# State space stage: tables in small portions, recurrence on VectorE, output units behind the last heads

## The chip, the cores and the metric

The kernel runs on one core of one Trainium2 chip. The metric is the device time of one execution in microseconds (us). All matrices are float32; each product is made of three matmuls on a rounded high part and the rest (`hi`, `lo`), so that weights are split on the chip before they are used.

## The reference

Two blocks of a model on 512 tokens of width 1024. The change lies in the first block's state space mixer (S5): 32 groups of 16 channels, each with 64 complex states.

```
proj = rmsnorm(x) @ w_in                  # u (512 wide), then q, k, v (512 each)
lam_bar = exp(lam * dt);  b_bar = ((lam_bar - 1) / lam) * b
states  = scan over tokens of  s = lam_bar * s + b_bar u
y = gelu(Re(c . states) + d * u)
y = y * sigmoid(y @ w_glu + b_glu)
mixed = concat(rmsnorm(y), rmsnorm(chunked_attention(q, k, v)))
x = x + mixed @ w_out;  x = x + FFN(rmsnorm(x));  x = rmsnorm(x)
```

Behind it come four layers of a second block, each with a mixer, attention on a memory of 256 vectors, and an FFN. The keys and values of that memory, for all four layers, are computed early in the kernel, between u and the first heads.

## The kernel before

The program is a list of units. A unit is 12 matmuls: four 128x128 weight tiles of one output tile, three matmuls each (`mm`, L185, L187, L189; 512 columns, 256 for the memory). Weights come in order through three buffers `raw` on SP's DMA queue, and are split two units ahead into `hi` (ScalarE, L233) and `lo` (VectorE, L235). Work beside the units is written as Python generators. Those in `self.gens` go one step on after each unit, those in `self.fine` one step after each matmul of a unit; a `yield` ends a step. The order in which instructions are issued this way is their priority; the tile framework then orders each engine's static queue by priority and by when it expects operands to be ready, so that an engine with nothing better to do takes later work early.

The units of the first block, counted from 0: 0 to 7 are u (four output tiles of two units), 8 to 39 the memory's keys and values (32 units), then heads in four pairs j of six units each (q, k, v), then w_out, and the FFN. The four units of GLU (`ssm_units`) stand before pair j = `SSM_AT`.

S5 runs in chunks of eight tokens beside these units:

- `s5_tables` (in `gens`): some 80 small VectorE operations on 16 to 64 columns, then `bb` (input matrices, 256 columns), powers `pw` of lam_bar up to 8, the block-diagonal `bd`, `L` (powers up to 64), and four blocks `A` of six operations on 512 columns (`cmul`, two of the blocks on GpSimd), turned by TensorE (L1224) into `Ain`.
- `s5_u`: copies u from PSUM, scales it by the norm (L1239) and stores it to DRAM.
- `s5_main` (in `fine`): waits for the tables, loads u, computes the chunks' states S (L1319, 128 small matmuls), then runs the recurrence over them, 14 steps of three operations on GpSimd (L1339 to L1341), `S5_STEP` matmuls apart.
- `s5_toeps` (in `fine`, beside the recurrence): clears two Toeplitz tiles, and for four parts m makes the powers F (`s5_powers`, 12 operations of 288 columns, L1260 to L1265), multiplies them (L1287), and spreads the result through DRAM into the Toeplitz tile (eight DMAs, L1299).
- `s5_main`, second part: `S5_WAIT` matmuls after both, four outputs: S is copied by GpSimd into S2 (L1352), 32 matmuls (L1358 with F, L1366 with the Toeplitz tile), y goes by way of `s5x` to DRAM (L1374, L1377). F for m = 2 and 3 is made a second time here, for half of it on GpSimd.

`s5x` has one buffer; F and A share two. `ssm_begin` ends whatever of `s5_main` is left, loads y turned and applies GELU (L1397); GLU's results are multiplied, squared, normed (L289, L323) and split again (`ssm_out`) before w_out can use them. `att_done` drains all generators before w_out.

Of the kernel before, what the change touches and what calls it, by code (L numbers as in the profile page):

```python
# [98 lines left out]
class Kern:  # L99
# [979 lines left out]
    def s5_tmp(self):  # L1079
        return self.s5.tile([P, T], F32, tag="s5x", name="s5x")  # L1080

    def s5_tables(self):
# [51 lines left out]
        dt = stt(acc, 1.0, kj.bitcast(F32), add, mul)  # L1134
        re, im = tt(lr, dt, mul), tt(li, dt, mul)
# [7 lines left out]
        r = ts(r, 3.1415925, -3.1415925, ALU.min, ALU.max)  # L1143
        s1, sh = new(16), new(16)
# [4 lines left out]
        em1 = stt(th, 2.0, rec, mul, mul)  # L1149
        mag = ts(em1, 1.0, None, add, ALU.bypass)  # L1150
# [13 lines left out]
        V.tensor_copy(out=pw[:, 1, :, 1:2], in_=ai.unsqueeze(2))  # L1164
        t = new(64).rearrange("p (a b) -> p a b", a=16)

        def cmul(out_r, out_i, xr, xi, yr, yi, t, eng):
            eng.tensor_tensor(out=out_r, in0=xr, in1=yr, op=mul)
            eng.tensor_tensor(out=t, in0=xi, in1=yi, op=mul)
            eng.tensor_tensor(out=out_r, in0=out_r, in1=t, op=sub)  # L1170
            eng.tensor_tensor(out=out_i, in0=xr, in1=yi, op=mul)
            eng.tensor_tensor(out=t, in0=xi, in1=yr, op=mul)
            eng.tensor_tensor(out=out_i, in0=out_i, in1=t, op=add)

        for lo, w in ((1, 1), (2, 2), (4, 4)):
            b = [pw[:, c, :, lo:lo + 1].to_broadcast([P, 16, w]) for c in (0, 1)]
            cmul(pw[:, 0, :, lo + 1:lo + 1 + w], pw[:, 1, :, lo + 1:lo + 1 + w],
                 pw[:, 0, :, 1:1 + w], pw[:, 1, :, 1:1 + w], b[0], b[1], t[:, :, :w], V)
# [5 lines left out]
        cmul(bb[:, 0], bb[:, 1], br, bi, w3[0], w3[1], t, V)  # L1184
        bd = pool.tile([P, 2, 16, 32], F32, tag="bd", name="bd")
        nc.gpsimd.memset(bd, 0.0)
        for c in range(2):
            for q in range(2):
                rows = slice(64 * q, 64 * q + 64)
                V.tensor_copy(out=bd[rows, c, :, 16 * q:16 * q + 16], in_=bb[rows, c])  # L1190
        pv = tail[:, 512:].rearrange("p (c a b) -> p c a b", c=2, a=16)
        for j in range(8):
            V.tensor_copy(out=pv[:, :, :, j:j + 1], in_=pw[:, :, :, 7 - j:8 - j])

# [4 lines left out]
        for w in (1, 2, 4):  # L1199
            b = [L[:, c, 0, :, w - 1:w].to_broadcast([P, 16, w]) for c in (0, 1)]  # L1200
            cmul(L[:, 0, 0, :, w:2 * w], L[:, 1, 0, :, w:2 * w], L[:, 0, 0, :, :w], L[:, 1, 0, :, :w],
                 b[0], b[1], t[:, :, :w], V)
# [7 lines left out]
        for m in range(4):  # L1210
            A = pool.tile([P, 2, 4, 9, 16], F32, tag="big", name="A", bufs=2)[:, :, :, 0:8]
            js = slice(4 * m, 4 * m + 4)
            x = [bb[:, c, js].unsqueeze(2).to_broadcast([P, 4, 8, 16]) for c in range(2)]
            y = [pv[:, c, js].unsqueeze(3).to_broadcast([P, 4, 8, 16]) for c in range(2)]
            t = (self.s5_tmp() if m % 2 else self.tmp()).rearrange("p (a b c) -> p a b c", a=4, b=8)
            cmul(A[:, 0], A[:, 1], x[0], x[1], y[0], y[1], t, G if m % 2 else V)
# [12 lines left out]
            yield  # L1229

    def s5_u(self, m, ps, norm):

        nc = self.nc
        t = self.tmp()
        turned = t.rearrange("p (t c) -> p c t", t=8)
        src = ps.rearrange("p (c t) -> p c t", t=8)

        nc.scalar.activation(out=turned, in_=src, func=ACTF.Copy)
        nc.vector.tensor_tensor(  # L1239
            out=turned, in0=turned, in1=self.bc(norm).rearrange("p (c t) -> p c t", t=8), op=ALU.mult,  # L1240
        )
# [5 lines left out]
    def s5_powers(self, m, split=(False, False)):  # L1247

        nc = self.nc
        cr, ci = self.s5_c  # L1250
        F = self.s5.tile([P, 2, 4, 9, 16], F32, tag="big", name="F", bufs=2)
        for q in range(2):
            js, ls = slice(4 * m + 2 * q, 4 * m + 2 * q + 2), slice(2 * q, 2 * q + 2)
            shape = [P, 2, 9, 16]
            x = [v[:, js].unsqueeze(2).to_broadcast(shape) for v in (cr, ci)]
            y = [self.s5_pw[:, c, js].unsqueeze(3).to_broadcast(shape) for c in range(2)]
            G = nc.gpsimd if split[q] else nc.vector
            t = (self.s5_tmp() if q else self.tmp())[:, :288]
            t = t.rearrange("p (a b c) -> p a b c", a=2, b=9)
            G.tensor_tensor(out=F[:, 0, ls], in0=x[0], in1=y[0], op=ALU.mult)  # L1260
            G.tensor_tensor(out=t, in0=x[1], in1=y[1], op=ALU.mult)
            G.tensor_tensor(out=F[:, 0, ls], in0=F[:, 0, ls], in1=t, op=ALU.subtract)
            G.tensor_tensor(out=F[:, 1, ls], in0=x[0], in1=y[1], op=ALU.mult)
            G.tensor_tensor(out=t, in0=x[1], in1=y[0], op=ALU.mult)
            nc.vector.scalar_tensor_tensor(  # L1265
                out=F[:, 1, ls], in0=F[:, 1, ls], scalar=-1.0, in1=t, op0=ALU.mult, op1=ALU.subtract
            )
        return F

    def s5_toeps(self):  # L1270
# [3 lines left out]
        for pair in (1, 0):  # L1274
            toep = self.toep[pair] = pool.tile([P, 8, 2, P], F32, tag="tab", name="toep", bufs=2)
            nc.vector.memset(toep, 0.0)
            k_dram = self.k_dram[pair]
            for m in range(2):
                ms = slice(8 * pair + 4 * m, 8 * pair + 4 * m + 4)
                F = self.powers[2 * pair + m] = self.s5_powers(2 * pair + m)  # L1280
# [11 lines left out]
                kt = self.s5_tmp()[:32].rearrange("p (j c) -> p j c", j=4)  # L1292
# [11 lines left out]
    def s5_main(self, tables):  # L1304
        nc = self.nc
        while tables in self.gens:
            yield
# [4 lines left out]
        S, G, L = self.S, nc.gpsimd, self.s5_L  # L1312
# [37 lines left out]
        for m in range(4):  # L1350
# [26 lines left out]
            nc.sync.dma_start(out=self.y_dram[m].rearrange("p g c -> p (g c)"), in_=y)  # L1377
            yield
# [94 lines left out]
    def first(self):  # L1473
# [12 lines left out]
        def squares():  # L1486
# [9 lines left out]
            self.finish(st["norm"]["gen"])  # L1496
# [291 lines left out]
```

## Time and profile before

| | us |
|---|---|
| three runs | 3168.74 median, 3168.13 to 3169.31 |
| the profiled execution | 3168.23 |
| its span, first to last instruction | 3166.3 |
| TensorE busy in the span | 3097.5 (98%) |
| VectorE busy | 1757.6 (56%) |
| GpSimd busy | 562.2 (18%) |

PE is TensorE, PEld its weight loads, DVE VectorE, ACT ScalarE, POOL GpSimd, SP the queue that issues the DMAs. Busy times of TensorE overlap from one matmul to the next. PEclk is the clock granted to TensorE as a share of 2.4 GHz, averaged over the stretch.

### The profile page before, as it was taken

Reading aid. Unit: us, or ns where it says so; the run is one execution under the profiler, and the core shown is the slowest. Engines: PE = TensorE matmul, PEld = TensorE weight load, DVE = VectorE, ACT = ScalarE, POOL = GpSimd, SP = SyncE. Lnnn points to the kernel's source line nnn. Section 1 sums busy time; section 2 is a strip of 40 time slices with the busy share of each in tenths; the row PEclk is TensorE's granted clock in tenths of the full one; section 3 lists DMA queues with packets and bytes.
Section 4 is the critical chain, followed back from the end, with each engine's and each line's share of the span. In section 5 each row is a group of like instructions: output and inputs, shape, how many; then the busy total and the mean of one; then the engine's idle time right before and its main releaser. Section 6 shows DMA issues by size and latency. Waiting matters only on the chain.

```text
span 3166.3 us, 39145 instructions
## 1 busy us (share of the span) xinstructions
PE 3097.5 (98%) x14664; PEld 2587.2 (82%) x14664; DVE 1757.6 (56%) x2979; ACT 1347.9 (43%) x2488; POOL 562.2 (18%) x464
## 2 busy tenths in 40 slices
PE   7899999999999999999999999999999999999998
PEld 6687788888888888888888888887888888878886
DVE  8977644458755344566753445655444477554444
ACT  5365423347754232455432334334333467542332
POOL 2731201032212010111110001112000123120103
PEclk9899999999999999999999999999999999999999
DMA  6432223332223323322233333233333322132332
GB/s 210 111 99 80 93 93 97 98 98 62 67 75 104 100 90 103 94 77 80 70 104 99 91 102 94 88 95 98 94 97 98 98 67 67 62 105 93 97 98 79
DMA packets 101694, 295.29 MB, mean 93 GB/s; under 512 B 22496, under 2 KB 26592, under 8 KB 101472
## 3 DMA queue, kind: packets, MB, share of 16 engines
q1 hardware_dynamic: 101504, 292.79, 30.4%
q8 instruction: 115, 1.88, 0.2%
q14 instruction: 75, 0.61, 0.1%
HBM read 286.20 MB, written 6.55 MB: 92 GB/s over the span
## 4 chain that ended last, share of the span: by engine, by line
PE 91%; DVE 6%; issue 1%; ACT 1%; DMA 1%; POOL 0%; SPq 0%; DVEq 0%; ACTq 0%; POOLq 0%
PE g L185 27%; PE g L189 27%; PE g L187 27%; DVE lo L235 1%; PE a L224 1%; PE a L225 1%; PE a L223 1%; DVE x L414 1%; PE z L722 1%; PE z L735 1%; PE a L289 0%; PE a L635 0%; PE z L187 0%; PE z L185 0%; PE z L189 0%
## 5 line engine op out<-in xcount | busy, mean ns | idle before, releaser
L233 ACT ACTIVATE hi<-raw 128x512 fp32r<-128x512 f32 (+2 forms) x1094 | 662.3, 607 | 1430.7 <-PE g L187 1330.4
L235 DVE TENSOR_TENSOR lo<-raw,hi 128x512 fp32r<-128x512 f32 (+2 forms) x1094 | 765.7, 701 | 653.8 <-ACT hi L233 643.7
L185 PE MATMUL g<-xh,hi 128*128 128x512 f32 x2720 | 1067.7, 393 | 12.2 <-ACT hi L233 7.8
L189 PE MATMUL g<-xh,lo 128*128 128x512 f32 x2720 | 1064.7, 392 | 0.0
L187 PE MATMUL g<-xl,hi 128*128 128x512 f32 x2720 | 1064.0, 391 | 0.0
L185 PEld LDWEIGHTS g<-xh,hi 128*128 128x128 f32 x2720 | 513.1, 189 | 119.8 <-ACT hi L233 7.8
L189 PEld LDWEIGHTS g<-xh,lo 128*128 128x128 f32 x2720 | 512.7, 188 | 105.2 <-issue 0.2
L187 PEld LDWEIGHTS g<-xl,hi 128*128 128x128 f32 x2720 | 512.9, 189 | 103.3
L189 PE MATMUL g<-ah,lo 128*128 128x512 f32 x1110 | 433.6, 391 | 3.1 <-DVE lo L235 2.7
L185 PE MATMUL g<-ah,hi 128*128 128x512 f32 x1110 | 432.0, 390 | 2.0 <-ACT t L271 2.0
L187 PE MATMUL g<-al,hi 128*128 128x512 f32 x1110 | 432.2, 389 | 0.0
L427 POOL TENSOR_TENSOR t<-t,bc 128x512 f32<-128x512 f32 x110 | 143.2, 1302 | 1405.2 <-ACT t L426 1405.2
L189 PEld LDWEIGHTS g<-ah,lo 128*128 128x128 f32 x1110 | 208.3, 188 | 50.8 <-DVE lo L235 8.0
L185 PEld LDWEIGHTS g<-ah,hi 128*128 128x128 f32 x1110 | 208.4, 188 | 45.3 <-ACT t L271 2.8
L187 PEld LDWEIGHTS g<-al,hi 128*128 128x128 f32 x1110 | 208.4, 188 | 43.1
L398 DVE TENSOR_TENSOR t<-g,bc 128x512 f32<-128x512 f32 x182 | 125.1, 688 | 173.7 <-PE g L189 169.5
L414 DVE TENSOR_TENSOR x<-x,g 128x512 f32<-128x512 f32 x151 | 103.4, 685 | 136.2 <-PE g L189 136.2
L429 DVE TENSOR_TENSOR t<-g,t 128x512 f32<-128x512 f32 x110 | 76.1, 692 | 180.3 <-PE g L189 160.4
L272 POOL TENSOR_TENSOR acc<-acc,t 128x512 f32<-128x512 f32 x82 | 114.9, 1405 | 335.9 <-ACT t L271 319.8
L233 ACT ACTIVATE ah<-t 128x512 fp32r<-128x512 f32 x110 | 69.5, 632 | 45.8 <-DVE t L429 45.8
L426 ACT ACTIVATE t<-t 128x512 f32<-128x512 f32 x110 | 69.7, 634 | 33.4 <-DVE t L398 33.3
L235 DVE TENSOR_TENSOR al<-t,ah 128x512 fp32r<-128x512 f32 x110 | 76.1, 692 | 12.0 <-ACT ah L233 2.3
(341 smaller groups left out, 3048.0 us busy)
## 6 DMA issues: line engine op xcount, KB each, us to landing
raw<-in_weights_dram SPq DMA_DIRECT2D x436, 512.0 KB, 3.5
raw<-in_weights_dram SPq DMA_DIRECT2D x76, 448.0 KB, 3.3
raw<-in_weights_dram SPq DMA_DIRECT2D x18, 384.0 KB, 3.2
x<-in_xT_dram SPq DMA_DIRECT2D x16, 256.0 KB, 3.6
x<-in_att_bias_dram SPq DMA_DIRECT2D x8, 256.0 KB, 6.0
kv<-kv SPq DMA_DIRECT2D x32, 64.0 KB, 2.4
out_dram<-x SPq DMA_DIRECT2D x8, 256.0 KB, 2.1
mraw<-in_memT_dram SPq DMA_DIRECT2D x2, 512.0 KB, 6.2
```

Of the source, the lines that this page charges most:

```text
L185: nc.tensor.matmul(out=out, lhsT=wh, rhs=xh, start=u.first and i == 0, stop=False)
L187: nc.tensor.matmul(out=out, lhsT=wh, rhs=xl, start=False, stop=False)
L189: nc.tensor.matmul(out=out, lhsT=wl, rhs=xh, start=False, stop=u.last and i == len(u.ks) - 1)
L223: nc.tensor.matmul(out=out, lhsT=ah, rhs=bh, start=start, stop=False)
L233: nc.scalar.activation(out=hi, in_=src, func=ACTF.Copy)
L235: eng.tensor_tensor(out=lo, in0=src, in1=hi.bitcast(F32), op=ALU.subtract)
L272: nc.gpsimd.tensor_tensor(out=norm["acc"][rows, :n], in0=norm["acc"][rows, :n], in1=sq[rows, :n], op=ALU.add)
L398: nc.vector.tensor_tensor(out=t, in0=ps, in1=bc, op=ALU.mult)
L414: self.nc.vector.tensor_tensor(out=self.x[m], in0=self.x[m], in1=ps, op=ALU.add)
L426: nc.scalar.activation(out=tg, in_=tg, func=ACTF.Silu)
L427: nc.gpsimd.tensor_tensor(out=tg, in0=tg, in1=self.bc(n), op=ALU.mult)
L429: nc.vector.tensor_tensor(out=h, in0=ps, in1=tg, op=ALU.mult)
```

## The change

`s5_tables` gives its operations out in some 37 steps instead of 11 (a `yield` after every few), `cmul` becomes a generator. `s5_powers` makes F in six operations of 576 columns on VectorE, `S5_PACE` = 6 matmuls apart, with the sign of c's imaginary part turned once in the tables. The recurrence's three operations go from GpSimd to VectorE, 14 matmuls apart instead of 10. The Toeplitz tiles are cleared by GpSimd. u is copied into x[4+m] and scaled as soon as the norm is there, and the norm is no longer forced to an end in `squares`. The GLU units stand behind all four head pairs (`SSM_AT` 4). With the same rule of counting, the tables end after unit 41 (before: 15).

```
-S5_STEP = 10
-S5_FILL = (24, 0)
-S5_POOL = (False, True)
+S5_STEP = 14
+S5_FILL = (12, 0)
+S5_PACE = 6
-SSM_AT = 3
+SSM_AT = 4
     def s5_tmp(self):
-        return self.s5.tile([P, T], F32, tag="s5x", name="s5x")
+        return self.s5.tile([P, 576], F32, tag="s5x", name="s5x")
     def s5_tables(self):
         f = stt(k, 2.12194440054690583e-4, f, mul, add)
+        yield
...
-        def cmul(out_r, out_i, xr, xi, yr, yi, t, eng):
+        def cmul(out_r, out_i, xr, xi, yr, yi, t, eng, pace=False):
             eng.tensor_tensor(out=out_r, in0=xr, in1=yr, op=mul)
             eng.tensor_tensor(out=t, in0=xi, in1=yi, op=mul)
+            if pace:
+                yield
...
-        cmul(bb[:, 0], bb[:, 1], br, bi, w3[0], w3[1], t, V)
+        yield from cmul(bb[:, 0], bb[:, 1], br, bi, w3[0], w3[1], t, V, True)
+        yield
+        V.tensor_scalar(out=ci, in0=ci, scalar1=-1.0, scalar2=None, op0=mul)
...
     def s5_u(self, m, ps, norm):
-        t = self.tmp()
+        t = self.x[4 + m]
         nc.scalar.activation(out=turned, in_=src, func=ACTF.Copy)
+        while norm["bc"] is None:
+            yield
...
+    def s5_powers(self, m, store, key):
+        F = store[key] = self.s5.tile([P, 2, 4, 9, 16], F32, tag="big", name="F", bufs=2)
+        js, shape = slice(4 * m, 4 * m + 4), [P, 4, 9, 16]
+        t = self.s5_tmp().rearrange("p (a b c) -> p a b c", a=4, b=9)
+        for c, op in ((0, ALU.add), (1, ALU.subtract)):
+            V.tensor_tensor(out=F[:, c], in0=x[c], in1=y[0], op=ALU.mult)
+            yield from wait(S5_PACE)
+            V.tensor_tensor(out=t, in0=x[1 - c], in1=y[1], op=ALU.mult)
+            yield from wait(S5_PACE)
+            V.tensor_tensor(out=F[:, c], in0=F[:, c], in1=t, op=op)
+            yield from wait(S5_PACE)
...
     def s5_toeps(self):
-            nc.vector.memset(toep, 0.0)
+            nc.gpsimd.memset(toep, 0.0)
-                F = self.powers[2 * pair + m] = self.s5_powers(2 * pair + m)
+                yield from self.s5_powers(2 * pair + m, self.powers, 2 * pair + m)
+                F = self.powers[2 * pair + m]
...
     def s5_main(self, before):
-            G.tensor_tensor(out=pr, in0=src.to_broadcast(shape), in1=fac, op=ALU.mult)
-            G.tensor_tensor(out=pr[:, :, 0:16], in0=pr[:, :, 0:16], in1=pr[:, :, 16:32], op=ALU.add)
-            G.tensor_tensor(out=dst, in0=dst, in1=pr[:, :, 0:16], op=ALU.add)
+            V.tensor_tensor(out=pr, in0=src.to_broadcast(shape), in1=fac, op=ALU.mult)
+            V.tensor_tensor(out=pr[:, :, 0:16], in0=pr[:, :, 0:16], in1=pr[:, :, 16:32], op=ALU.add)
+            V.tensor_tensor(out=dst, in0=dst, in1=pr[:, :, 0:16], op=ALU.add)
             yield from wait(S5_STEP)
...
-            if m < 2:
-                self.powers[m + 2] = self.s5_powers(m + 2, S5_POOL)
             nc.sync.dma_start(out=self.y_dram[m].rearrange("p g c -> p (g c)"), in_=y)
+            if m < 2:
+                yield from self.s5_powers(m + 2, self.powers, m + 2)
             yield
...
         def squares():
             self.begin_norm(st["norm"], D, 1e-6, gap=0)
-            self.finish(st["norm"]["gen"])
             yield
...
         def u_post(m, ps):
-            self.s5_u(m, ps, st["norm"])
+            st["u", m] = self.spawn(self.s5_u(m, ps, st["norm"]))
+            next(st["u", m], None)
             if m == 3:
-                st["s5"] = self.spawn(self.s5_main(st["tables"]), self.fine)
+                before = [st["u", k] for k in range(4)] + [st["tables"]]
+                st["s5"] = self.spawn(self.s5_main(before), self.fine)
```

## Rows read from the trace of the kernel before

**Rows 1.** The page: busy time, share of the span and instructions of each engine.

```profile
PE 3097.5 (98%) x14664; PEld 2587.2 (82%) x14664; DVE 1757.6 (56%) x2979; ACT 1347.9 (43%) x2488; POOL 562.2 (18%) x464
```

**Rows 2.** Busy time by stage: length, engines (instructions), PEclk, DMA share, GB/s.

```profile
0.00:50.00 50.00, 30.82 (x122) 24.98 (x122) 42.86 (x139) 28.72 (x50) 15.04 (x16) 0.91 0.63 216
50.00:85.00 35.00, 34.15 (x268) 33.94 (x268) 33.57 (x64) 15.32 (x27) 12.28 (x9) 0.93 0.64 196
85.00:143.00 58.00, 43.57 (x362) 37.64 (x361) 54.75 (x68) 15.81 (x26) 43.78 (x37) 0.85 0.40 103
143.00:226.00 83.00, 81.64 (x480) 69.84 (x478) 67.47 (x140) 49.40 (x104) 32.83 (x33) 1.00 0.36 105
226.00:273.00 47.00, 41.11 (x200) 34.39 (x200) 33.94 (x59) 35.54 (x61) 11.00 (x8) 0.96 0.27 79
273.00:335.00 62.00, 58.23 (x263) 47.76 (x264) 46.76 (x87) 29.05 (x60) 11.55 (x8) 0.94 0.26 81
...
380.00:400.00 20.00, 20.00 (x90) 16.54 (x89) 8.86 (x14) 7.59 (x12) 2.57 (x2) 1.00 0.30 92
```

**Rows 3.** Waits of TensorE, 0 to 362 us: total, times, longest.

```profile
PE a L323 <- DVE t L309: 11.4, 2, 6.2
...
PE s5ps L1287 <- DVE F L1265: 7.6, 3, 5.7
```

**Rows 4.** Groups of VectorE, 60 to 140 us: busy, mean ns, idle before.

```profile
L235 DVE TENSOR_TENSOR lo<-raw,hi 128x512 fp32r<-128x512 f32 x30 | 29.0, 977 | 1.1 <-ACT hi L233 1.1
...
L551 DVE TENSOR_TENSOR kvt<-g,membc 128x256 f32<-128x256 f32 x14 | 5.7, 410 | 0.0
...
L1276 DVE MEMSET toep<- 128x2048 f32 x2 | 3.5, 1765 | 0.7 <-issue 0.7
```

**Rows 5.** Groups of VectorE, 360 to 500 us.

```profile
L235 DVE TENSOR_TENSOR lo<-raw,hi 128x512 fp32r<-128x512 f32 x52 | 35.8, 688 | 40.7 <-ACT hi L233 40.7
```

**Rows 6.** One line, L1265: count, shortest/median/longest ns, first and last start.

```profile
L1265 DVE SCALAR_TENSOR_TENSOR F<-F,t x6: 444/764/1760, 89.3 to 197.5; 128x288 f32<-128x288 f32 x6
```

**Rows 7.** Groups of GpSimd, 0 to 230 us.

```profile
L1339 POOL TENSOR_TENSOR pr<-S,s5p 128x512 f32<-128x512 f32 x14 | 20.7, 1480 | 6.0 <-ACT S L1325 5.0
L1341 POOL TENSOR_TENSOR S<-S,pr 128x256 f32<-128x256 f32 x14 | 14.6, 1043 | 0.9
L1340 POOL TENSOR_TENSOR pr<-pr 128x256 f32<-128x256 f32 x14 | 14.0, 999 | 1.1
...
L272 POOL TENSOR_TENSOR acc<-acc,t 128x512 f32<-128x512 f32 x3 | 4.0, 1337 | 5.2 <-ACT t L271 5.2
```

**Rows 8.** TensorE in order of time, the memory's units: start, duration.

```profile
57.06 0.28 PE L185 MATMUL g<-memh,hi 128*128 128x256 f32 x1
57.18 0.28 PE L187 MATMUL g<-meml,hi 128*128 128x256 f32 x1
...
130.18 0.28 PE L189 MATMUL g<-memh,lo 128*128 128x256 f32 x1
```

**Rows 9.** SP's queue in order of time.

```profile
162.42 4.83 SPq L1299 DMA_DIRECT2D toep<-k_dram  x8
```

**Rows 10.** TensorE in order of time, the first S5 output.

```profile
171.02 0.61 PE L1358 MATMUL s5ps<-S,F 128*128 128x128 f32 x4
...
174.14 0.56 PE L1366 MATMUL s5ps<-U,toep 128*128 128x64 f32 x4
```

**Rows 11.** All engines in order of time, from the last S5 output to w_out.

```profile
218.45 0.60 ACT L1374 ACTIVATE s5x<-s5ps 128x512 f32<-128x512 f32 x1 [1.77 <-PE s5ps L1366]
...
227.90 0.99 PE L185 MATMUL g<-yh,hi 128*128 128x512 f32 x3 [1.96 <-ACT yh L233]
...
246.20 0.40 PE L189 MATMUL g<-yh,lo 128*128 128x512 f32 x1
...
273.15 1.65 PE L185 MATMUL g<-yh,hi 128*128 128x512 f32 x3 [2.56 <-ACT yh L233]
```

More of the change, by code (lines that the diff above doesn't have):

```diff
@@ L1143, in s5_tables @@
         r = ts(r, 3.1415925, -3.1415925, ALU.min, ALU.max)
+        yield
         s1, sh = new(16), new(16)
@@ L1149, in s5_tables @@
         em1 = stt(th, 2.0, rec, mul, mul)
+        yield
         mag = ts(em1, 1.0, None, add, ALU.bypass)
@@ L1154, in s5_tables @@
         ar = tt(tt(em1, cos, mul), cm1, add)
+        yield
         den = tt(tt(lr, lr, mul), tt(li, li, mul), add)
@@ L1157, in s5_tables @@
         V.reciprocal(out=rec, in_=den)
+        yield
         wr = tt(tt(tt(ar, lr, mul), tt(ai, li, mul), add), rec, mul)
+        yield
         wi = tt(tt(tt(ai, lr, mul), tt(ar, li, mul), sub), rec, mul)
+        yield
         pw = keep(2, 16, 9)
@@ L1164, in s5_tables @@
         V.tensor_copy(out=pw[:, 1, :, 1:2], in_=ai.unsqueeze(2))
+        yield
         t = new(64).rearrange("p (a b) -> p a b", a=16)
-        def cmul(out_r, out_i, xr, xi, yr, yi, t, eng):
+        def cmul(out_r, out_i, xr, xi, yr, yi, t, eng, pace=False):
             eng.tensor_tensor(out=out_r, in0=xr, in1=yr, op=mul)
             eng.tensor_tensor(out=t, in0=xi, in1=yi, op=mul)
+            if pace:
+                yield
             eng.tensor_tensor(out=out_r, in0=out_r, in1=t, op=sub)
             eng.tensor_tensor(out=out_i, in0=xr, in1=yi, op=mul)
+            if pace:
+                yield
             eng.tensor_tensor(out=t, in0=xi, in1=yr, op=mul)
@@ L1176, in s5_tables @@
             b = [pw[:, c, :, lo:lo + 1].to_broadcast([P, 16, w]) for c in (0, 1)]
-            cmul(pw[:, 0, :, lo + 1:lo + 1 + w], pw[:, 1, :, lo + 1:lo + 1 + w],
-                 pw[:, 0, :, 1:1 + w], pw[:, 1, :, 1:1 + w], b[0], b[1], t[:, :, :w], V)
+            yield from cmul(pw[:, 0, :, lo + 1:lo + 1 + w], pw[:, 1, :, lo + 1:lo + 1 + w],
+                            pw[:, 0, :, 1:1 + w], pw[:, 1, :, 1:1 + w], b[0], b[1], t[:, :, :w], V)
+            yield
         tail = pool.tile([P, 3 * 256], F32, tag="kt", name="tail")
@@ L1190, in s5_tables @@
                 V.tensor_copy(out=bd[rows, c, :, 16 * q:16 * q + 16], in_=bb[rows, c])
+        yield
         pv = tail[:, 512:].rearrange("p (c a b) -> p c a b", c=2, a=16)
@@ L1193, in s5_tables @@
             V.tensor_copy(out=pv[:, :, :, j:j + 1], in_=pw[:, :, :, 7 - j:8 - j])
+        yield
         L = self.s5p[:, 48:560].rearrange("p (a c b k) -> p a c b k", a=2, c=2, b=16)
@@ L1200, in s5_tables @@
             b = [L[:, c, 0, :, w - 1:w].to_broadcast([P, 16, w]) for c in (0, 1)]
-            cmul(L[:, 0, 0, :, w:2 * w], L[:, 1, 0, :, w:2 * w], L[:, 0, 0, :, :w], L[:, 1, 0, :, :w],
-                 b[0], b[1], t[:, :, :w], V)
+            yield from cmul(L[:, 0, 0, :, w:2 * w], L[:, 1, 0, :, w:2 * w], L[:, 0, 0, :, :w],
+                            L[:, 1, 0, :, :w], b[0], b[1], t[:, :, :w], V)
+            yield
         V.tensor_scalar(out=L[:, 0, 1], in0=L[:, 1, 0], scalar1=-1.0, scalar2=None, op0=mul)
@@ L1214, in s5_tables @@
             y = [pv[:, c, js].unsqueeze(3).to_broadcast([P, 4, 8, 16]) for c in range(2)]
-            t = (self.s5_tmp() if m % 2 else self.tmp()).rearrange("p (a b c) -> p a b c", a=4, b=8)
-            cmul(A[:, 0], A[:, 1], x[0], x[1], y[0], y[1], t, G if m % 2 else V)
+            t = (self.s5_tmp()[:, :T] if m % 2 else self.tmp()).rearrange("p (a b c) -> p a b c", a=4, b=8)
+            yield from cmul(A[:, 0], A[:, 1], x[0], x[1], y[0], y[1], t, G if m % 2 else V, m % 2 == 0)
             yield
@@ L1238, in s5_u @@
         nc.scalar.activation(out=turned, in_=src, func=ACTF.Copy)
+        while norm["bc"] is None:
+            yield
         nc.vector.tensor_tensor(
@@ L1245, in s5_u @@
         )
-    def s5_powers(self, m, split=(False, False)):
-        nc = self.nc
+    def s5_powers(self, m, store, key):
+        V = self.nc.vector
         cr, ci = self.s5_c
[L1251 to L1268, printed above, removed]
+        F = store[key] = self.s5.tile([P, 2, 4, 9, 16], F32, tag="big", name="F", bufs=2)
+        js, shape = slice(4 * m, 4 * m + 4), [P, 4, 9, 16]
+        x = [v[:, js].unsqueeze(2).to_broadcast(shape) for v in (cr, ci)]
+        y = [self.s5_pw[:, c, js].unsqueeze(3).to_broadcast(shape) for c in range(2)]
+        t = self.s5_tmp().rearrange("p (a b c) -> p a b c", a=4, b=9)
[6 more added lines that the diff above has]
+            yield from wait(S5_PACE)
     def s5_toeps(self):
@@ L1291, in s5_toeps @@
                         yield
-                kt = self.s5_tmp()[:32].rearrange("p (j c) -> p j c", j=4)
+                kt = self.s5_tmp()[:32, :T].rearrange("p (j c) -> p j c", j=4)
                 nc.scalar.activation(out=kt, in_=ps, func=ACTF.Copy)
@@ L1302, in s5_toeps, with s5_main @@
                 )
-    def s5_main(self, tables):
+    def s5_main(self, before):
         nc = self.nc
-        while tables in self.gens:
+        while any(g in self.gens for g in before):
             yield
@@ L1311, in s5_main @@
         )
-        S, G, L = self.S, nc.gpsimd, self.s5_L
+        S, G, V, L = self.S, nc.gpsimd, nc.vector, self.s5_L
         G.memset(S[:, :, :, 0:1], 0.0)
@@ L1370, in s5_main @@
                     yield
-            if m < 2:
-                self.powers[m + 2] = self.s5_powers(m + 2, S5_POOL)
-            y = self.s5_tmp()
+            y = self.s5_tmp()[:, :T]
             nc.scalar.activation(
```

1 line of the change is left out of this document (added).

## Prediction

> **What bounds the kernel now.** I read the page first: TensorE is busy 98% of the span [rows 1], so the time can only move where it stands still or runs at its lower clock level. The table by stages says where: from 360 us on TensorE is busy 20.00 us of 20 at clock 1.00, so there is nothing to gain there. The first 335 us hold the losses [rows 2]. Per stage: idle 19.2, 0.9, 14.4, 1.4, 5.9 and 3.8 us, 45.5 us in all, of which 7.8 us are the first loads. The clock is 0.91, 0.93, 0.85, 1.00, 0.96 and 0.94 of the full level; of 58 us at 0.85, some 17 us ran at 1.2 GHz instead of 2.4, and lost up to half of that.
>
> In the two stages from 0 to 143 us VectorE is the bound: 42.9 of 50, 33.6 of 35 and 54.8 of 58 us busy. The waits of TensorE name it: 11.4 us for the two broadcasts of a norm, 7.6 us for the powers F [rows 3]. But much of that is not VectorE's work. The split `lo`, the same 128x512 operation, takes 977 ns between 60 and 140 us and 688 ns from 360 to 500 us [rows 4, 5]; a power operation of 288 columns takes 444 ns at least and 764 at the median [rows 6]. In 85 to 143 us GpSimd is busy 43.8 of 58 us [rows 2], with the recurrence above all: 42 instructions, 20.7 + 14.6 + 14.0 = 49.3 us [rows 7]. The operation `kvt`, which has one input in PSUM, stays at 410 ns through all this [rows 4]. So GpSimd's reading stretches VectorE's two-input operations.
>
> From 143 to 226 us TensorE is full (81.6 of 83) and VectorE has room (67.5). That room is what the change uses.
>
> **Part by part.** *A, 0 to 50 us.* The tables' small operations are issued some at a time, behind the splits, the norm is no longer forced, and u waits in x[4+m]. The longer of the two broadcast waits [rows 3] is 6.2 us, with table operations between its steps. I take -4 us; bounds 0 (the scheduler fills VectorE's gaps with whatever is ready, tables too) and -9 (most of 11.4). The `att_bias` loads into x[4] to x[7] now stand behind u's stores in SP's queue, and the weight loads behind them; with three raw buffers I count 0, and up to 3 us if u is late.
>
> *B, 50 to 143 us.* Counting yields by the code, the tables end after unit 41 in place of unit 15. Units 8 to 39 are the memory keys and values, so S5's state matmuls, powers and recurrence move behind these, into the heads. What stays is 32 units of 12 matmuls, 0.12 us apart [rows 8], 46 us, and an estimated 8 us of transposes; before, these units end at 130.5 us [rows 8], and by 143 two units of heads are through too. VectorE needs for the 32 units some 25 us (32 splits of 0.60 to 0.69 and 16 `kvt`), the rest of the tables some 22, and the two table blocks left on GpSimd stretch it by some 9: 56 us against 54 of TensorE. So this stage, which loses 14.4 us idle and up to 9 by the clock, nearly fills. I take -20 us of the 23; bounds -10 (tables and the stretch bind as now) and -23.
>
> *C, the heads.* Here VectorE gets the recurrence: 14 steps of one operation of 512 and two of 256 columns, 14 x (0.69 + 0.41 + 0.41) = 21 us [rows 4, 5]. The powers are 6 operations of 576 columns in place of 12 of 288: from 0.44 us at 288 and 0.69 at 512, an estimate of 0.75 each, 4.5 us a call, 18 us for the four calls of `s5_toeps`. One head costs TensorE some 25 us (72 matmuls, 90 in 20 us, so 16 us, and 8 to 9 of attention: 81.6 us in 143 to 226 are some 2.7 heads and 15 of S5 outputs), VectorE some 19 (67.5 us for about three heads, less the late powers, 14 at the median of 0.76 [rows 2, 6]). Up to the last head's units: VectorE 3.5 x 19 + 21 + 18 + some 5 of stretch = 111 us, TensorE 100. The stage is lengthened by what VectorE lacks. I take +8 us against the 1.4 lost now; bounds 0 (work is pulled ahead into B) and +20 (both engines near full wait for each other). The two Toeplitz memsets, 1.77 us each [rows 4], leave VectorE for GpSimd: some -3 us, in the 111 already.
>
> The Trainium skill, in SBUF — State Buffer, section Who interferes with whom, says that a VectorE operation with two SBUF inputs contends with a GpSimd instruction that reads SBUF, not with one that only writes; by it those memsets cost VectorE nothing, and if they stretched it like the recurrence the sum would be some 2 us worse. The unstretched `kvt` agrees with the half of the rule on one SBUF input; no row above shows a memset.
>
> *D, the tail.* Now the GLU units come before head 3, whose matmuls hide the norm of y, and w_out's state-space half hides head 3's attention. After, behind the last head's matmuls stand in a row: the last Toeplitz block with its eight DMAs (4.83 us of issue) [rows 9], some 6 us; the four S5 outputs, 3.7 us of matmul each [rows 10]; GLU; y's norm. Between the outputs all goes through one buffer s5x (y out, its DMA, the powers' t, the next y): about 25 us for the four. From y's copy at 218.5 to the first GLU matmul at 227.9 it is 9.4 us; GLU is 48 matmuls, 11 us; from GLU's end at 246.6 to the first w_out matmul at 273.2 it is 26.6 us now, with steps placed late: sigmoid, product, square, sum, rsqrt, two broadcasts, scaling and split alone, at 0.6 to 1.4 us each as operations of that size here, I estimate at 15 us [rows 5, 7, 11]. Then w_out, 192 matmuls, 44 us, of which up to three banks (8 us) can run ahead on the finished heads. Together 6 + 25 + 9 + 11 + 2 (half clock) + 15 + 44 - 8 = 104 us, with 80 us of TensorE work (S5 14.5, last attention 8.5, GLU 11, w_out 44, sums 2): 24 us lost. Now 5.9 + 3.8 idle, 3 to 5 of clock, and gaps that overlapping records hide, some 20 lost. I take +4 us; bounds -10 (the S5 outputs are pulled into the heads) and +20 (they start later than 6 us behind).
>
> The Trainium skill, in TensorE: Matmul & The Clock Gate, Part 1, says that the throttled state is the default and activity lifts it; by that an uncovered tail costs more than its idle time. Here the rows agree: 2.6 us of waiting at 273 [rows 11] stand in a stage with clock 0.94 [rows 2]. With S5's small matmuls at half rate too the sum would be some 7 us higher.
>
> **Sum.** -4 - 20 + 8 + 4 = -12 us. The profiled execution took 3168.2 us (span 3166.3 and 1.9 around it), 0.5 below the median of the three runs, 3168.7; so 3168.2 - 12 = 3156 us.
>
> **Rivals.** *It gains far more.* VectorE is relieved more than I count (powers halve in number, the recurrence's stretch goes), C costs 0 and the outputs are pulled ahead: -4 - 22 + 0 - 6 = -32 us, 3136. For it: TensorE stays full in the heads today with VectorE at 81%. Against it: 39 us of new work against 15 us of room.
>
> *Nothing moves.* The gain of B is only carried into C: both engines must still do the same work by the last head, and 111 us of VectorE become 120: -3 - 17 + 16 + 4 = 0, 3168. For it: VectorE is over 90% busy throughout 0 to 143 us already.
>
> *Slower: the tail stands open.* One mechanism: the last F and Toeplitz block come late on a full VectorE, the S5 outputs wait for them, and with SSM_AT at 4 there is no head left to hide it. Each us that the first output starts later than some 6 us behind the last head's matmul is one us. It decides from 18 us on (the 12 of the forecast); at 30 us late: -12 + 24 = +12, 3180. For it: 7.6 us of waits on F today; against it: powers are issued from the first head's end on.
>
> **How the numbers follow.** Forecast -6 to -25: 0.42, its own range 3143 to 3162. Far more: 0.20. Nothing: 0.15. Slower: 0.23. About 0.2%, 6 us, is what a measurement of this kernel can tell from no change. So faster 0.62, same 0.15, slower 0.23. The range reaches into both outer cases, 3138 to 3175.
>
> **What would show it.** Right: the memory units end near 105 us in place of 130.5, the stretch 85 to 143 loses few us, `lo` there back toward 0.7 us; VectorE over 90% busy in the heads; three idle stretches between the last head and w_out (before GLU, behind GLU, at the Toeplitz load); the FFN begins some 12 us earlier. Wrong: the memory units still end after 120 us (B), heads longer than 125 us (C), or w_out starting later than 60 us behind the last head's matmul, less what it ran ahead (D).

## The result, and the profile after

The changed kernel takes 3186.8 us (median of four runs, 3185.23 to 3189.03), the kernel before beside it 3169.02: ratio 1.0056, 95% interval 1.0041 to 1.007. It is slower by some 18 us where I forecast 12 us faster. The profiled execution took 3185.2 us, 29 more than the 3156 forecast.

Busy time by stage of the kernel after, as in [rows 2] (length, then PE, PEld, DVE, ACT, POOL, then the granted clock, DMA share, GB/s):

```profile
50.00:85.00 35.00, 33.02 (x264) 32.84 (x265) 30.68 (x73) 13.87 (x23) 10.68 (x7) 0.95 0.75 229
85.00:143.00 58.00, 58.00 (x398) 44.48 (x396) 39.30 (x75) 30.42 (x60) 14.33 (x9) 1.00 0.35 103
143.00:226.00 83.00, 74.50 (x389) 60.38 (x387) 82.27 (x166) 42.71 (x92) 17.98 (x9) 0.96 0.27 78
226.00:273.00 47.00, 30.31 (x187) 27.21 (x188) 22.85 (x51) 18.70 (x38) 10.63 (x11) 0.80 0.27 66
273.00:335.00 62.00, 51.05 (x216) 40.99 (x215) 35.49 (x58) 25.87 (x43) 7.53 (x6) 0.90 0.22 64
```

The stage from 85 to 143 us now loses nothing (58.00 of 58 at clock 1.00, 43.57 at 0.85 before), and VectorE has only 39.3 us to do there instead of 54.8. From 143 to 226 us VectorE is full, 82.3 of 83. Then the gain is paid back: TensorE stands idle for 8.5, 16.7 and 11 us in the last three stages, at clock 0.96, 0.80 and 0.90, where before 1.4, 5.9 and 3.8 us were lost.

The longest waits of TensorE that bear on the change, 0 to 380 us (total, times, longest), to be read against [rows 3]:

```profile
PE g L185 <- ACT yh L233: 10.7, 2, 9.3
...
PE a L289 <- POOL acc L272: 6.3, 1, 6.3
PE s5ps L1307 <- DVE F L1286: 6.3, 1, 6.3
...
PE a L323 <- DVE t L309: 2.8, 2, 1.6
```

The norm's broadcasts cost 2.8 us instead of 11.4. The wait ahead of GLU has grown from 2.0 us [rows 11] to 9.3, and one of 6.3 us behind GLU, for the sum of y's squares, is new. The waits on F were 7.6 us in three pieces among the memory units; now it is one of 6.3 us behind the last head's matmul.

The way to the end, from the timeline of the kernel after (start, duration; rows of several engines):

```profile
97.64 0.28 PE L189 MATMUL g<-memh,lo 128*128 128x256 f32 x1
...
207.75 0.39 PE L189 MATMUL g<-xh,lo 128*128 128x512 f32 x1
...
215.71 3.19 PE L1307 MATMUL s5ps<-F,bd 128*32 128x128 f32 x14 [6.25 <-DVE F L1286]
...
224.05 6.27 SPq L1319 DMA_DIRECT2D toep<-k_dram  x8
...
226.55 0.41 DVE L1361 TENSOR_TENSOR S<-S,pr 128x256 f32<-128x256 f32 x1
...
234.96 0.66 PE L1378 MATMUL s5ps<-S,F 128*128 128x128 f32 x4
...
260.35 0.56 PE L1386 MATMUL s5ps<-U,toep 128*128 128x64 f32 x4
260.99 0.60 ACT L1392 ACTIVATE s5x<-s5ps 128x512 f32<-128x512 f32 x1 [4.29 <-PE s5ps L1386]
...
270.19 1.65 PE L185 MATMUL g<-yh,hi 128*128 128x512 f32 x3 [9.29 <-ACT yh L233]
...
285.30 0.39 PE L189 MATMUL g<-yh,lo 128*128 128x512 f32 x1
...
301.49 0.96 PE L185 MATMUL g<-yh,hi 128*128 128x512 f32 x3 [1.43 <-ACT yh L233]
```

The memory units end at 97.9 us (130.5 in [rows 8]) and the last of the heads' q, k and v matmuls (from here on "the last head's matmul") at 208.1; attention of the last heads follows it. But the last K matmuls (L1307, which multiply F) wait for F until 215.7, the last Toeplitz block is issued at 224.1 to 230.3, and the recurrence ends at 227.0. The first S5 output starts at 235.0, 26.9 us behind the last head's matmul ([rows 10]: 171.0, with a head still to come), and GLU at 270.2 instead of 227.9 [rows 11]. TensorE isn't idle through all of the 26.9 us: 9.7 us are waits, the rest is the K matmuls and the last heads' attention, which stands in its queue right up to the first output.

### The profile page after: what moved, and what is told of

It is laid out like the page before. It is cut to its first block, busy times and chain, and to the rows that moved or that the text cites. A ratio compares the mean times of both kernels' runs of the same rounds, so it can differ in the third digit from the quotient of the medians.

```text
span 3183.4 us, 39113 instructions
## 1 busy us (share of the span) xinstructions
PE 3107.4 (98%) x14664; PEld 2588.1 (81%) x14664; DVE 1747.2 (55%) x2994; ACT 1345.1 (42%) x2486; POOL 515.5 (16%) x414
## 4 chain that ended last, share of the span: by engine, by line
PE 91%; DVE 6%; ACT 1%; issue 1%; DMA 0%; POOL 0%; DVEq 0%; SPq 0%; ACTq 0%; POOLq 0%
PE g L185 27%; PE g L189 27%; PE g L187 27%; DVE lo L235 1%; PE a L224 1%; PE a L225 1%; PE a L223 1%; PE z L722 1%; DVE x L414 1%; PE z L735 1%; PE a L289 0%; PE a L635 0%; PE z L189 0%; PE z L187 0%; PE z L185 0%
## 5 line engine op out<-in xcount | busy, mean ns | idle before, releaser
L235 DVE TENSOR_TENSOR al<-t,ah 128x512 fp32r<-128x512 f32 x110 | 76.1, 692 | 11.6 <-ACT ah L233 2.3
```

The costliest lines, as they stand in the source:

```text
L235: eng.tensor_tensor(out=lo, in0=src, in1=hi.bitcast(F32), op=ALU.subtract)
```

## The experiments

Three theories stood at the start. *Theory 1, late chain:* the S5 outputs start late because the recurrence and the Toeplitz blocks are put off onto a full VectorE, and each us of it is one us. *Theory 2, open tail:* output units behind the last heads cost by themselves. *Theory 3:* the recurrence on VectorE costs more than the stretch that it removes.

**1. Output units ahead of head 3 again (`a_ssm3`).** The Toeplitz work is finished first there.

```diff
-SSM_AT = 4
+SSM_AT = 3
...
+            self.finish(self.toeps)
             self.finish(st["s5"])
```

> The changed kernel (3186.8 us) with SSM_AT = 3 alone, the Toeplitz generator ended by force before the GLU units. Late chain (theory 1: the state space outputs start 27 us behind the last head's matmuls because recurrence and Toeplitz blocks were moved late on a full VectorE, and each us of that is one us): head 3's 16 us of matmuls and the norm's 15 us cover each other again, and the chain gets ahead of head 3 in priority: 3165 to 3175. Open tail (theory 2: GLU behind the heads costs by itself, whenever the outputs start): 3165 to 3172, the same here. VectorE (theory 3: the recurrence on VectorE costs more than it took from VectorE on GpSimd): 3182 to 3190, the place of GLU hardly matters.

Measured: 3198.01 us, 1.0088 (1.0073 to 1.0103), worse than the change whole. S5 outputs from 221 to 249.6 us, GLU at 258.7, with head 3 behind it. All three ranges miss, theory 3's by 8 us. The outputs are still late, as theory 1 has it, but head 3 doesn't cover that: it now stands behind them.

**2. Recurrence back on GpSimd (`a_rec_pool`).**

```diff
-            V.tensor_tensor(out=pr, in0=src.to_broadcast(shape), in1=fac, op=ALU.mult)
+            G.tensor_tensor(out=pr, in0=src.to_broadcast(shape), in1=fac, op=ALU.mult)
...
```

> The changed kernel with the recurrence's three operations back on GpSimd, nothing else. Late chain: GpSimd needs 49 us for what VectorE does in 21, and stretches VectorE meanwhile; the outputs start as late or later: 3185 to 3200. Open tail: 3182 to 3190, since GLU stays behind the heads. VectorE (theory 3): VectorE has 21 us less to do in the heads, the outputs start earlier: 3165 to 3176.

Measured: 3189.8 us, 1.0059 (1.0044 to 1.0074). The recurrence now ends at 189 us, but the K matmuls only at 225, and the first S5 output still starts at 231. Theory 3 falls: taking the recurrence away from VectorE gains nothing while the other chain, F to K to Toeplitz block, is as late. VectorE's operations are longer beside it (`lo` 929 ns on average from 98 to 228 us, 750 after), and the last head's matmul ends at 227.7 instead of 208.1. So the first output stands only 3.4 us behind it, and yet the time is the same: what counts is when the outputs come, not how far behind the heads.

**3. Tables three, then two steps at a time (`a_every3`, `a_every2`).** All else as after.

```diff
+def every(g, n):
+    for i, _ in enumerate(g):
+        if i % n == 0:
+            yield
...
-            st["tables"] = self.spawn(self.s5_tables())
+            st["tables"] = self.spawn(every(self.s5_tables(), 3))
```

> The changed kernel, its tables issued three steps at a time, so that they end after about unit 14 in place of 41; everything else, GLU behind the heads too, stays. Late chain: states, powers and recurrence spread from the memory's units on, the outputs are done before the last head ends, and GLU follows it at once: the FFN begins 15 to 40 us earlier than in the changed kernel, 3145 to 3170. Open tail: GLU (11 us) and y's norm (15 us) remain uncovered: 3176 to 3184. VectorE: 3180 to 3190.

> The kernel after, with the tables' steps issued two at a time instead of one (three at a time gave 3154.7 us and a first S5 output at 175 us, one at a time 3186.8 and 235). Theory 1 (late chain: each microsecond by which the S5 outputs come too late for the units that could cover it is one microsecond): tables end near the 21st memory unit, first S5 output at 195 to 210 us, whole 3158 to 3174 us. Theory 2 (the open tail costs by itself, the same in every kernel with the output units last): the price is fixed, so the time stays near that of three at a time, 3152 to 3158 us, as long as the last S5 output is ahead of the last head's last unit, and jumps to 3180 to 3188 else.

Measured: 3154.7 us, 0.9951 (0.9934 to 0.9967), and 3154.2, 0.9947 (0.993 to 0.9963). The two are the fastest here, 16 us better than before and 32 better than the change. Three at a time lies in theory 1's range. Two at a time lies in theory 2's (3152 to 3158), and theory 1's began 4 us higher; but theory 2 wanted the last S5 output ahead of the last head's matmul, and it ends at 225.5 us against 217.3. The step is not gradual, as I had expected of two at a time: in both, the states' matmuls fall among the memory units (86 to 94 us) as before (85 to 91), while one at a time puts them behind (105 to 130 us). Those matmuls and the recurrence's first operations (count, shortest/median/longest ns, first and last start), after, then two at a time:

```profile
L1339 PE MATMUL a<-U,Ain x128: 222/222/271, 104.9 to 130.2; 128*64 128x64 f32 x128
L1359 DVE TENSOR_TENSOR pr<-S,s5p x14: 672/888/1159, 132.5 to 223.2; 128x512 f32<-128x512 f32 x14
```

```profile
L1345 PE MATMUL a<-U,Ain x128: 222/222/270, 85.9 to 92.1; 128*64 128x64 f32 x128
L1365 DVE TENSOR_TENSOR pr<-S,s5p x14: 668/1082/1791, 94.3 to 165.1; 128x512 f32<-128x512 f32 x14
```

And the stages 50 to 140 and 140 to 226 us, after, then two at a time:

```profile
50.00:140.00 90.00, 88.02 (x647) 76.12 (x648) 67.04 (x140) 41.36 (x77) 25.01 (x16) 0.98 0.50 150
140.00:226.00 86.00, 77.50 (x401) 61.58 (x399) 85.21 (x174) 45.64 (x97) 17.98 (x9) 0.96 0.28 80
```

```profile
50.00:140.00 90.00, 86.41 (x678) 77.79 (x679) 88.49 (x161) 38.56 (x65) 24.57 (x16) 0.97 0.52 155
140.00:226.00 86.00, 84.49 (x505) 73.33 (x504) 78.93 (x170) 50.60 (x114) 19.84 (x18) 1.00 0.32 92
```

That is the cause in one column: after, VectorE works 67.0 of 90 us in the first stretch and 85.2 of 86 in the second; two at a time, 88.5 and 78.9. Some 21 us of VectorE's work is put off from a stretch in which it then idles into one in which it is full.

**4. Recurrence on VectorE alone, in the kernel before (`b_rec_vector`).** Experiment 2 the other way round.

> The kernel before (3169 us) with the recurrence on VectorE, that part of the change alone. Late chain and open tail: VectorE gets 21 us and loses the stretch of 49 us of GpSimd beside it, and the recurrence ends before 150 us in place of 163: 3155 to 3170. VectorE (theory 3): slower, 3174 to 3185.

Measured: 3179.25 us, 1.0028 (1.0019 to 1.0037). Memory units end at 117 us instead of 130, three heads at 187 instead of 221. But the S5 outputs come at 187 to 230 us instead of 171 to 218, and TensorE stands ahead of GLU, which is placed before head 3, until they are there:

```profile
239.55 1.65 PE L185 MATMUL g<-yh,hi 128*128 128x512 f32 x3 [9.15 <-ACT yh L233]
```

A gain of 34 us in the heads became a loss of some 8, because GLU starts 11.7 us later (227.9 before). Theory 3 had the number here, but not the reason: the heads got faster with the recurrence on VectorE, and the gain is lost because the outputs come later than GLU's place asks for.

**5. Three steps at a time, output units ahead of head 3 (`a_every3_ssm3`).** Experiments 1 and 3 together.

> The kernel after with the tables three steps at a time, and the S5's output units ahead of head 3's pairs again, as in the kernel before. Theory 1: the place of the output units doesn't matter while the S5 outputs are in time; but they come at 175 to 216 us here and the third head pair ends near 197, so TensorE waits some 10 to 20 us ahead of the GLU and gets back the 24 us that it stood between GLU and w_out: 3145 to 3160 us. Theory 2 (the open tail has a price of its own, some 15 us): 3135 to 3146 us.

Measured: 3165.05 us, 0.9981 (0.9972 to 0.9991), 10 us slower than with the units last. Theory 2 falls: the place behind the heads, with its open tail, is the better one once the heads are this fast. Theory 1's range was 5 us too low; GLU starts at 220.6.

**6. Output units last, alone (`b_ssm4`),** SSM_AT = 4 in the kernel before.

> The kernel before with one part of the change alone: the S5's output units behind the last heads. Its S5 outputs are all there at 218 us, far ahead of the heads' end, so nothing is late. Theory 1 (only lateness costs): 3165 to 3173 us. Theory 2 (the open tail costs by itself: between the GLU's last matmul and w_out's first nothing is left to cover ssm_out's chain, 24 us in the kernel with tables three at a time, against about 10 us from the last head to w_out before): 3178 to 3190 us.

Measured: 3171.21 us, 1.0001 (0.9991 to 1.001), in theory 1's range. The S5 outputs end at 218 us and the heads at 243, so nothing is late, and the place costs nothing that can be measured. GLU moves from 227.9 to 250.5, and the 23 us of head 3 that stood behind it are gone.

**7. A faster pace of what follows the tables (`a_pace`).**

```diff
-S5_STEP = 14
-S5_FILL = (12, 0)
-S5_PACE = 6
+S5_STEP = 4
+S5_FILL = (0, 0)
+S5_PACE = 1
```

> The kernel after with its tables as they are, and the pace of what follows them raised: 4 units between recurrence steps instead of 14, 1 between power operations instead of 6, none of the 12 ahead of the K matmuls. Theory 1 (pacing makes the chain late): recurrence and Toeplitz blocks end 20 to 35 us earlier, the S5 outputs start at 195 to 215 us, 3155 to 3170 us. Rival (VectorE is full from 140 to 220 us, 19.8 of each 20 us, so what is moved ahead pushes the heads back by as much): the heads end 8 to 15 us later, 3172 to 3185 us.

Measured: 3191.59 us, 1.0065 (1.005 to 1.008). The K matmuls end 13 us earlier, but the recurrence 6 us later (last operation at 232.7), and VectorE is as full as in the kernel after (85.0 of 86 us in 140 to 226). It is not the pace: on a full VectorE one chain only takes the other's place. The rival was right that a full VectorE gives nothing back, but it was the recurrence that was pushed back: the last head's matmul ends at 211.1, 3 us later and not 8 to 15. Its range was 7 us too low.

**8. Two parts together in the kernel before (`b_rec_ssm4`):** the edits of 4 and 6.

> The kernel before with two parts of the change together: the recurrence on VectorE and the output units behind the last heads (alone they gave 1.0028 and 1.0001). Theory 1, as it now stands (TensorE stands wherever the output units are placed ahead of the S5 outputs that they need; a faster heads' stage is worth its gain only if the output units come after): with the recurrence on VectorE alone the GLU stood 9 us, and head 3 behind it; with the units moved, 3150 to 3162 us. Rival (the parts add up): 3178 to 3182 us.

Measured: 3172.82 us, 1.0011 (1.0002 to 1.002), in neither range. The S5 outputs start at 187, 207, 226 and 234 us and end at 238, 18 behind the last head's matmul, with the powers of the kernel before between them, so GLU starts only at 248.6. Theory 1's number is 11 us too low: with these two parts the outputs are still late, which it did not foresee.

**9. Two steps at a time, recurrence on GpSimd (`a_every2_pool`).**

> The kernel after with tables two steps at a time, and the recurrence back on GpSimd. If the recurrence on VectorE is what makes the memory units and the heads faster once nothing is late: 3162 to 3172 us, with memory units ending near 125 us and VectorE's 256- and 512-column operations beside GpSimd's stretched again. If the gain is the new tables, powers and u alone: 3150 to 3158 us.

Measured: 3168.99 us, 0.9995 (0.9985 to 1.0004): with nothing put off, the recurrence on VectorE is worth 15 us. The range is met, but not by way of the memory units, which end at 110.5 us and not near 125 (108.4 with the recurrence on VectorE); the last head's matmul ends at 228.7 instead of 217.3. VectorE's groups, 60 to 140 us (busy, mean ns, idle before), two at a time, then the same with GpSimd:

```profile
L241 DVE TENSOR_TENSOR lo<-raw,hi 128x512 fp32r<-128x512 f32 x33 | 28.7, 875 | 0.2 <-ACT hi L239 0.2
L557 DVE TENSOR_TENSOR kvt<-g,membc 128x256 f32<-128x256 f32 x13 | 5.3, 411 | 0.0
```

```profile
L241 DVE TENSOR_TENSOR lo<-raw,hi 128x512 fp32r<-128x512 f32 x30 | 31.5, 1059 | 0.3 <-ACT hi L239 0.2
L557 DVE TENSOR_TENSOR kvt<-g,membc 128x256 f32<-128x256 f32 x13 | 5.4, 414 | 0.0
```

**10. Two steps at a time, S5 outputs held back (`a_every2_late`).** The recurrence ends at 169 us and the K matmuls at 160; only the outputs are put behind the heads.

```diff
-S5_WAIT = 100
+S5_WAIT = 2000
```

> The kernel after with tables two steps at a time (3154.2 us; first S5 output at 176 us, last at 225, the heads' last unit at 217), but with the S5 outputs held back by 2000 units, which puts them all behind the last heads, where the recurrence and the Toeplitz blocks are long done. Nothing is late then but the place of the output units: four S5 outputs of 25 us in all, 9 us to the GLU. Theory 1: TensorE stands for what no longer lies beside the heads, and the GLU starts near 252 us instead of 238: 3163 to 3170 us; the kernel after then owes the rest of its 32 us to the 18 us by which its recurrence ends behind the heads. Theory 2 (the place alone makes the kernel after slow): 3180 to 3190 us.

Measured: 3163.59 us, 0.9982 (0.9972 to 0.9991). The first output starts at once behind the last head's matmul, and GLU at 246.5:

```profile
203.71 0.48 PE L195 MATMUL g<-xh,lo 128*128 128x512 f32 x1
204.02 0.61 PE L1384 MATMUL s5ps<-S,F 128*128 128x128 f32 x4
...
246.51 0.80 PE L191 MATMUL g<-yh,hi 128*128 128x512 f32 x1 [8.04 <-DMA t<-y_dram]
```

All four outputs behind the heads cost 9.4 us against two at a time. The other 23 us up to the kernel after are work that ends late: its heads end 4 us later, and its first output starts 26.9 us behind them instead of at once; its four outputs then take 26 us instead of 32.5.

**11. The states' matmuls in a row (`a_states_row`),** the kernel after otherwise.

```diff
                             rhs=self.U[:, m, q, jj], start=True, stop=True,
                         )
-                    yield
```

> The kernel after, its tables one step at a time as they are, with one change: the 160 matmuls of the S5 states are issued in a row, not one group at a time between two matmuls of a head. Between heads a group of them took 0.47 us, in a row 0.13 us, so the states end some 12 us earlier (near 118 us instead of 130), and the recurrence starts as much earlier, while VectorE still idles. Theory 1 (VectorE's work is put off into the stretch in which it is full): the recurrence ends 8 to 15 us earlier and so does all behind it, 3172 to 3180 us. Rival (what counts is the S5's Toeplitz chain alone): 3184 to 3189 us.

(The trace has 128 such matmuls; the 160 above counted some twice.) Measured: 3174.31 us, 1.0014 (1.0005 to 1.0023), as theory 1 had it. 128 of them take 3.95 us in a row:

```profile
104.30 3.95 PE L1339 MATMUL a<-U,Ain 128*64 128x64 f32 x128
```

The recurrence starts at 111.2 us instead of 132.5, VectorE is busy 78.7 of 90 us from 50 to 140 instead of 67.0, the last S5 output ends at 248.4 instead of 260.9, and the time falls by the same 12.5 us.

**All of them in one table.** Times in the span from the traces; the last column is the median less GLU's start.

| kernel | last S5 output ends | GLU starts | median us | difference |
|---|---|---|---|---|
| *head 3 behind GLU* | | | | |
| before | 218 | 227.9 | 3169.0 | 2941 |
| b_rec_vector | 230 | 239.6 | 3179.3 | 2940 |
| a_ssm3 | 250 | 258.7 | 3198.0 | 2939 |
| a_every3_ssm3 | 211 | 220.6 | 3165.1 | 2944 |
| *no head behind GLU* | | | | |
| a_every3 | 216 | 231.9 | 3154.7 | 2923 |
| a_every2 | 225 | 235.6 | 3154.2 | 2919 |
| a_every2_pool | 236 | 246.1 | 3169.0 | 2923 |
| a_every2_late | 236 | 246.5 | 3163.6 | 2917 |
| b_rec_ssm4 | 238 | 248.6 | 3172.8 | 2924 |
| b_ssm4 | 218 | 250.5 | 3171.2 | 2921 |
| a_states_row | 248 | 257.9 | 3174.3 | 2916 |
| after | 261 | 270.2 | 3186.8 | 2917 |
| a_rec_pool | 263 | 272.3 | 3189.8 | 2918 |
| a_pace | 265 | 274.9 | 3191.6 | 2917 |

Over 43 us of GLU's start the rest is 2916 to 2924 us, or 2939 to 2944 with a head behind it. GLU starts 9 to 11 us behind the last S5 output, save in `a_every3` and `b_ssm4`, where the heads end later than that. So the first 270 us come down to one number: when the last S5 output is there, or the heads' end where that is later.

## Why the prediction was wrong

*A and B, right in kind, and larger than said.* The units of u end at 38 us instead of 44, and the memory units at 97.9 instead of 130.5, forecast near 105; the 27 us that the second gains on the first are more than B's bound of 23. The stage that I called nearly full loses nothing. One sign did not come: `lo` takes 852 ns in 85 to 143 us (1001 before), not some 0.7 us.

*C, right in its number, by luck.* From the memory units to the last head's matmul I forecast 111 us, all of them VectorE's work; it is 110.2. But VectorE was busy for 93.6 us of these only:

```profile
97.90:132.50 34.60, 34.60 (x235) 23.97 (x234) 18.57 (x33) 15.59 (x30) 6.98 (x4) 1.00 0.29 88
132.50:208.10 75.60, 75.21 (x388) 59.97 (x387) 75.03 (x156) 42.53 (x92) 14.13 (x7) 1.00 0.29 82
```

Until the recurrence starts at 132.5 us it stands idle for 16 us, and then it is full. What it hadn't done at 208.1, two operations of the last F and more than three of the recurrence's 14 steps, fell to D. Of C's terms the powers came out (0.75 us an operation undisturbed, 19.5 us in all for 18), and the recurrence was too small: 26.7 us for 21.

*D, the step that failed.* I put the tail at 104 us behind the last head's matmul, w_out's last matmul included; it is 141:

| term | forecast | measured |
|---|---|---|
| to the first S5 output | 6 | 26.9 |
| the four S5 outputs | 25 | 25.9 |
| to GLU | 9 | 9.3 |
| GLU, with half clock | 13 | 15.5 |
| GLU to w_out | 15 | 15.8 |
| w_out, less what runs ahead | 36 | 47.6 |

Four terms held to within 3 us. The failing one is the first: the last Toeplitz block with its eight DMAs, "some 6 us". It takes for granted that F and the recurrence are through when the last head's matmul is. I had costed C as if VectorE's 111 us were shared so that S5 and heads end together, but TensorE's heads did not wait for S5: they ended at 208.1 with the last F at 215.7 and the recurrence at 227.0. The work that I had moved out of B was the same that D waits for. And even with F in time, 6 us were too few: from F to the end of the block's issue it is 14.7 us: the K matmuls, then a copy, a sum and a store to DRAM, and only then the eight DMAs (6.3 us of issue, not 4.8). In the 4.6 us from there to the first output the block lands and TensorE works off the attention ahead of it; which of the two set the start, the profile doesn't say. By the prediction's own sign for D, w_out starting later than 60 us behind the last head's matmul, it fails clearly: it starts 93 us behind. The second failing term is the last: w_out was to run 8 us ahead on the finished heads, but between GLU's end and 301.5 us TensorE's queue holds the sums and broadcasts of y's norm and the last head's attention, and nothing of w_out; with 3.6 us more behind its start this adds 11.6 us.

The balance: w_out's last matmul ends at 333 us before; less 12 and less 104 my forecast had the last head's matmul at 217. It came 9 us earlier, the tail is 37 us longer, together 28 of the 29 us.

*The rival "the tail stands open"* was the right mechanism, with a chance of 0.23, and its row was the right one to watch: the wait on F. By its rule, 20.9 us beyond 6 make -12 + 20.9 = +8.9, 3177 us; the other tail terms add 16 and the early heads take 9, which is the 3185 measured within 1 us. What I held against it, that powers are issued from the first head's end on, was true and beside the point: issued is not done on a VectorE that is full. The experiments price the parts: 23 us for what ends late (10), 9 us for the outputs' place behind the heads (10), against 15 us that the recurrence on VectorE gives when nothing is late (9).

*The stretch by GpSimd*, on which B rests, is shown: with the recurrence on GpSimd `lo` takes 1059 ns on average, on VectorE 875, while `kvt`, with one input in PSUM, takes 414 and 411. The Trainium skill, in SBUF — State Buffer, section Who interferes with whom, names VectorE operations with two SBUF inputs as those that contend with a GpSimd instruction that reads SBUF; the trace agrees. That GpSimd's memsets cost VectorE nothing, which the prediction drew from the same section, experiment 10 shows. Five power operations run beside the two memsets at 0.71 to 0.76 us each; beside the recurrence on GpSimd (9) the same lines take 1.07 to 1.33 us on average. VectorE and GpSimd, two at a time with the outputs held back:

```profile
89.54 3.67 POOL L1301 MEMSET toep<- 128x2048 f32 x2 [1.90 <-PE a L1345]
89.83 0.76 DVE L1292 TENSOR_TENSOR F<-F,s5x 128x576 f32<-128x576 f32 x1
90.50 1.42 DVE L1288 TENSOR_TENSOR F<-s5p,s5t 128x576 f32<-128x576 f32 x2
91.84 0.75 DVE L1290 TENSOR_TENSOR s5x<-s5p,s5t 128x576 f32<-128x576 f32 x1
92.63 0.76 DVE L1292 TENSOR_TENSOR F<-F,s5x 128x576 f32<-128x576 f32 x1
```

*What stays open.* Two steps at a time is 18.6 us faster than the two parts of experiment 8. How much of that is the spread tables, the wider powers or the way u is scaled was not taken apart; with the recurrence on GpSimd all three together give some 2 us, hardly clear of noise (9 against 6), so in these runs they pay only beside the recurrence on VectorE. Nor was it tried why one at a time puts the states behind the memory units and two doesn't; by the code the tables' steps are counted in units, and the 41 that they need reach past the last memory unit, the 39th.

## What to carry to other kernels

Spreading an engine's work thin is a gain only if the chain that the work feeds is still through before its consumer stands alone: compare the engine's busy time in the stretch it leaves with that in the stretch it goes to, and look for what is queued at the end of the chain. When an order is fixed by hand, find the one start on which all else hangs (here GLU's), and cost every edit by what it does to that start. The best version here is the change with its tables issued two or three steps at a time, 3154 us.

## What the runs showed of the hardware

Small matmuls between large ones cost several times what they cost in a row. After, four of the states' 64-column matmuls stand between two of 512 columns, and this pattern repeats every 0.70 us:

```profile
110.10 0.51 PE L189 MATMUL g<-xh,lo 128*128 128x512 f32 x1
110.53 0.34 PE L1339 MATMUL a<-U,Ain 128*64 128x64 f32 x4
110.80 0.51 PE L185 MATMUL g<-xh,hi 128*128 128x512 f32 x1
```

A 512-column matmul among its like comes every 0.23 us, so the four cost 0.47 us; in a row they cost 4 x 3.95 / 128 = 0.12 us. TensorE shows as full all that time. The Trainium skill, in TensorEngine Tiling (Array Packing), section Tiling Modes, says that a change of the tiling mode drains TensorE; the rows, 128*64 tiles between 128*128, agree with it, at 0.35 us for the two changes, but no run here parts the drain from other costs of mixing.

An uncovered tail runs at half rate in part only. Four stretches of the kernel after (length, PE, PEld, DVE, ACT, POOL, granted clock, DMA share, GB/s), then the longest matmuls of the third S5 output and one of GLU's first:

```profile
229.70:232.20 2.50, 2.50 (x8) 2.31 (x9) 2.40 (x9) 1.71 (x7) 0.00 (x0) 0.50 0.34 68
235.00:238.60 3.60, 3.60 (x35) 3.60 (x34) 1.02 (x2) 1.27 (x2) 1.26 (x1) 1.00 0.00 0
250.50:255.00 4.50, 4.50 (x26) 4.50 (x27) 2.14 (x3) 0.50 (x1) 1.26 (x1) 0.62 0.17 62
270.20:275.00 4.80, 4.80 (x11) 3.79 (x12) 2.08 (x3) 4.71 (x6) 0.00 (x0) 0.50 0.00 0
...
251.57 1.17 PE L1378 MATMUL s5ps<-S,F 128*128 128x128 f32 x4
...
271.64 0.63 PE L187 MATMUL g<-yl,hi 128*128 128x512 f32 x1
```

A clock of 0.50 is the 1.2 GHz level. The first S5 output, with TensorE busy for 5 us right ahead of it, runs at the full level, and four of its matmuls take 0.66 us (0.61 in [rows 10]). The third, behind 2.3 us of standing still, runs in part at the lower level, with up to 1.17 us for four; all of its matmuls take 5.4 us, the first output's 3.7. GLU's first ones, behind 9.3 us of standing still, take 0.63 us each, later ones 0.39. Of the 7 us that the prediction set against S5's small matmuls at half rate, some 2 came.

VectorE's time for one shape is not one number either, even with GpSimd idle. The recurrence's first seven steps take longer than its last seven, here the first operation of a step from either part in experiment 10, where GpSimd does nothing from 93.2 to 127.5 and from 130.5 to 150.9 us:

```profile
107.50 1.14 DVE L1365 TENSOR_TENSOR pr<-S,s5p 128x512 f32<-128x512 f32 x1
...
141.02 0.67 DVE L1365 TENSOR_TENSOR pr<-S,s5p 128x512 f32<-128x512 f32 x1
```

The third operation takes 0.63 to 0.66 us there and 0.40 to 0.42 later. By the code the first seven steps read and write S eight elements apart, the last seven take neighbours; no run changes that alone. It is most of why the 21 us that C counted for the recurrence became 26.7.
